# The low parts of the query, key and value weight splits: from GpSimd to VectorE

## The chip, the cores and the metric

The kernel runs on one core of one Trainium2 chip. The metric is the device time of one execution in microseconds, from runs on the chip; one further execution was taken with the hardware profiler, and every row below is from it. Engines are named as in the profile: PE is TensorE, PEld its weight loads, DVE is VectorE, ACT is ScalarE, POOL is GpSimd, SP is SyncE.

## The reference, cut to what matters

A decoder trunk of two layers on 512 tokens of width 1024, all in float32. Each layer is a mixer (three kinds of attention on 16 heads of 64) and a mixture of experts (32 experts, top 2 in one group of 8).

```python
for l in range(DEPTH):
    mod = cond @ ada_w[l] + ada_b[l]                      # six vectors of 1024
    h = rmsnorm(x, norm1_g[l]) * (1.0 + sc1) + sh1
    u = h @ w_in[l]                                       # queries, keys, values, gates
    o_a, o_b, o_c = nsa(...), fox(...), stick_breaking(...)
    x = x + g1 * (rmsnorm_per_head(concat(o_a, o_b, o_c)) @ w_out[l])
    h = rmsnorm(x, norm2_g[l]) * (1.0 + sc2) + sh2
    x = x + g2 * hier_moe(h, ...)
```

The change touches only `h @ w_in`. The kernel makes that product in split form: each float32 matrix is written as a high part (rounded to the `fp32r` type) and a low part (the difference), and three matmuls (high by high, high by low, low by high) replace one.

## The kernel before, in words

**Stages of a layer.** First `ln1` (line 530) normalizes x, transposes it on PE and splits it into `h` (high and low). Then the mixer runs a list of steps written out by hand, `ORDER` (one string for each layer, lines 102 to 105). A step is half a query/key projection (`q0` to `q7`, `proj_qk`, line 597), half a value projection (`v0` to `v2`, `proj_v`, line 675), one unit of an attention (`sb`, `fox`, `nsa`), a piece of the modulation (`ada`), or a piece of the output projection (`p..`, `w..`, `t.`). Projections and attention units are interleaved, so that PE has matmuls while ACT and DVE work on an attention unit. After the mixer comes the mixture of experts (`experts`, line 1315), which streams 1 MB weight tiles.

**How an engine's order comes about.** The framework orders the instructions of each engine when the program is built, from the order in which the code emits them and from what they depend on. Each engine then runs its own list strictly in that order: an instruction that waits for a semaphore holds all that stand behind it on its engine.

**The split of a weight.** `split` (line 282) makes the high part with a cast, on ACT by default (line 283), and the low part with a subtraction, on DVE by default (line 284; `le` names another engine). Line 284 is therefore the line of every low part in the profile, and the tile names tell them apart: `wl` are the low parts of the query/key weights (`split_qk`, line 583), `vl` those of the value weights (`split_v`, line 637), `wol` those of the output weights (`wo_parts`, line 1090), `h` those of the normalized input, `q`, `k`, `hilo` and `oh` others. A projection step of `qk` needs two pairs (`wh`, `wl`) of 128x512; a value projection needs four pairs (`vh`, `vl`) of 128x512. All of them take turns in 8 buffers of the tag `W`, so a cast into a buffer waits until PE has read what lay there. The split for the second half of a projection is emitted right behind the first half's matmuls (line 611), one step ahead of its use.

In the kernel before, `wl` is made on DVE only for `q7` and `q6` of the first layer and `vl` on DVE only for `v2` of the first layer; all the others are made on POOL. POOL also makes the low parts `wol` (always) and half of the `h` (line 564), one multiplication of the rotary embedding (line 626), and some additions of the modulation (line 382).

**An attention unit.** `scores` (line 790, matmuls on line 797) writes S in PSUM, in one of two double banks. For `sb` (line 1008) follow three ACT passes (lines 1018 to 1020), a DVE operation that reads S (line 1021), two DVE scans (line 1023), a DVE subtraction that reads S again (line 1025) and an ACT pass (line 1026). For `fox` and `nsa`, `softmax` (line 816) is a DVE maximum, ACT exponentials and DVE scalings. Then PE transposes the result (line 864) and ACT or DVE copies it out of PSUM (lines 278, 280).

Of the kernel before, what the change touches and what calls it, by code (L numbers as in the profile page):

```python
# [113 lines left out]
class K:  # L114
# [468 lines left out]
    def split_qk(self, l, c, s, he=None, le=None):  # L583
        w = self.get("wqk", l, c)[:, s]
        parts = []
        for h in range(2):
            wh = self.t4("W", [128, 4, 128], F32R, "wh")
            wl = self.t4("W", [128, 4, 128], F32R, "wl")
            self.split(wh, wl, w[:, 4 * h:4 * h + 4, :], he=he, le=le or (self.nc.vector if l == self.layers[0] and c > 5 else self.nc.gpsimd))
            parts.append((wh, wl))  # L590
        if s:
            self.done("wqk", l, c)
        return parts
# [43 lines left out]
    def split_v(self, l, g):  # L637
        parts = []
        for j in range(0, NK, 2):
            w = self.get("wv", l, g)  # L640
            if l != self.layer:
                x = self.t4("L", [128, 2, 2, 256], F32R, "vhl")
                wh, wl = x[:, 0], x[:, 1]
            else:
                wh = self.t4("W", [128, 2, 256], F32R, "vh")
                wl = self.t4("W", [128, 2, 256], F32R, "vl")
            he = None
            le = self.nc.vector if g == 2 and l == self.layers[0] else self.nc.gpsimd
            self.split(wh, wl, w[:, j:j + 2, :], he=he, le=le)
            parts.append((wh, wl))  # L650
        self.done("wv", l, g)
        return parts
# [999 lines left out]
```

## Time and profile before

| What | us |
|---|---|
| device time, median of 3 runs | 1844.76 |
| the three runs | 1836.57, 1845.58, 1844.76 |
| the profiled execution, device time | 1839.93 |
| its span, first to last instruction | 1838.0 |
| mean granted TensorE clock, of full speed | 0.965 |

How to read what follows: a busy time is the sum of an engine's own instructions; a wait is idle time of an engine just before an instruction, put down to the instruction whose semaphore came last. The granted clock is a share of full speed; this chip grants two levels, 1.2 and 2.4 GHz, which the table of stages shows as 0.5 and 1.0 where a stretch has one of them alone.

### The profile page before, as it was taken

The page shows a single profiled execution, that of the slowest core. Times are in us where ns is not written, and L with a number is a line of the kernel's source. Part 1 is how long each engine was busy: PE and PEld are TensorE (multiplying, and loading weights), DVE is VectorE, ACT ScalarE, POOL GpSimd, SP SyncE. Part 2 cuts the span into 40 slices and gives each one's busy share as a digit, 9 for nine tenths or more (in the row PEclk, how much of TensorE's full clock was granted, in tenths as well). Part 3 has the DMA queues.
Part 4 walks back from the last instruction along what each step waited for, and adds up shares of the span by engine and source line. Part 5 has one row for each costly group of instructions (what it writes and reads, how often), then busy time and mean ns, then how long its engine had stood idle before and what let it go on. Part 6 is the DMA issues. An engine that isn't in the chain of part 4 may idle for free. (4 is left out here: it accounts for less than half of the span.)

```text
span 1838.0 us, 24077 instructions
## 1 busy us (share of the span) xinstructions
PE 1742.5 (95%) x9126; PEld 917.2 (50%) x9126; DVE 970.0 (53%) x2022; ACT 663.1 (36%) x1526; POOL 235.3 (13%) x193
## 2 busy tenths in 40 slices
PE   6999999998999999999989999999979999999996
PEld 3766755655333433333356776566533343333333
DVE  2465367767344444333374975777634444344335
ACT  3565434345322222222245543445532222222222
POOL 1341412110000000000043332211000000000000
PEclk8998999999999999999999999899989999999998
DMA  7522374314999999999933244411399999999994
GB/s 293 208 92 90 113 292 153 123 46 176 384 420 420 419 420 420 420 421 420 419 144 138 91 141 151 157 62 53 149 354 411 419 420 421 420 420 420 420 421 196
DMA packets 78823, 512.64 MB, mean 279 GB/s; under 512 B 11000, under 2 KB 12280, under 8 KB 20080
## 3 DMA queue, kind: packets, MB, share of 16 engines
q1 hardware_dynamic: 72336, 496.77, 67.1%
q0 software_dynamic: 5216, 10.09, 1.5%
q10 hardware_dynamic: 1152, 4.19, 0.6%
q8 instruction: 75, 1.23, 0.3%
q14 instruction: 44, 0.36, 0.1%
HBM read 512.05 MB, written 6.29 MB: 282 GB/s over the span
## 5 line engine op out<-in xcount | busy, mean ns | idle before, releaser
L1387 PE MATMUL up<-ring_w,xeT 128*64 128x512 f32 x2048 | 461.7, 599 | 8.8 <-DMA ring_w<-in_expert_w 8.7
L1387 PEld LDWEIGHTS up<-ring_w,xeT 128*64 128x64 f32 x2048 | 139.2, 137 | 298.3 <-issue 250.7
L1417 PE MATMUL down<-ring_w,hT 128*64 128x512 f32 x1024 | 247.5, 605 | 0.8 <-DMA ring_w<-in_expert_w 0.8
L1395 ACT ACTIVATE F<-up,small 128x512 f32<-128x512 f32 x64 | 44.0, 687 | 461.1 <-PE up L1387 447.9
L609 PE MATMUL pj<-h,wh 128*128 128x512 f32 x512 | 167.1, 407 | 0.0
L466 DVE TENSOR_TENSOR x<-x,sc 128x512 f32<-128x512 f32 x256 | 159.3, 683 | 3.5 <-PE sc L1448 3.3
L1440 DVE TENSOR_SCALAR S<-sb,cf 128x512 fp32r<-128x512 f32 x64 | 47.9, 751 | 204.4 <-PE sb L1438 203.5
L283 ACT CAST Yh<-us 64x512 fp32r<-64x512 f32 x128 | 79.1, 618 | 197.4 <-DVE us L1428 189.7
L1362 POOL DMA_INDIRECT xr<-rows,index x32 | 31.9, 996 | 748.5 <-PE xg L1371 708.0
L1448 PE MATMUL sc<-Yh,S 128*128 128x512 f32 x256 | 110.2, 431 | 8.8 <-ACT z L1499 8.8
L797 PE MATMUL S<-k,q 64*128 64x512 f32 (+3 forms) x576 | 106.4, 399 | 8.5 <-DVE sbc L1025 5.2
L1417 PEld LDWEIGHTS down<-ring_w,hT 128*64 128x64 f32 x1024 | 62.2, 136 | 101.6 <-issue 87.6
L609 PEld LDWEIGHTS pj<-h,wh 128*128 128x128 f32 x512 | 96.1, 192 | 23.2 <-issue 1.2
L824 ACT ACTIVATE Pm<-S,sm_m 128x128 f32<-128x128 f32 (+3 forms) x160 | 83.0, 525 | 62.9 <-DVE sm_m L821 59.5
L1428 DVE TENSOR_TENSOR us<-down,gb 128x512 f32<-128x512 f32 x64 | 44.3, 692 | 116.3 <-PE down L1417 116.3
L1448 PE MATMUL sc<-Yl,S 128*128 128x512 f32 x256 | 103.7, 405 | 0.0
L609 PE MATMUL pj<-h,wl 128*128 128x512 f32 x256 | 102.5, 403 | 0.0
L1375 ACT ACTIVATE xeT<-xg,mods 128x128 f32<-128x128 f32 x256 | 95.5, 460 | 10.2 <-PE xg L1371 10.2
L284 POOL TENSOR_TENSOR wl<-ring_wqk,wh 128x512 fp32r<-128x512 f32 x56 | 74.8, 1349 | 167.1 <-ACT wh L283 161.3
L284 DVE TENSOR_TENSOR Yl<-us,Yh 64x512 fp32r<-64x512 f32 x128 | 87.3, 682 | 2.0
L821 DVE TENSOR_REDUCE sm_m<-S 128x2 f32<-128x256 f32 (+3 forms) x80 | 65.4, 820 | 36.7 <-PE S L797 35.8
L1448 PEld LDWEIGHTS sc<-Yh,S 128*128 128x128 f32 x256 | 49.6, 194 | 67.7 <-issue 58.3
(332 smaller groups left out, 2612.8 us busy)
## 6 DMA issues: line engine op xcount, KB each, us to landing
ring_w<-in_expert_w SPq DMA_DIRECT2D x384, 1024.0 KB, 19.8
ring_ada_sc<-in_ada_w SPq DMA_DIRECT2D x16, 1024.0 KB, 4.8
ring_ada_sh<-in_ada_w SPq DMA_DIRECT2D x16, 1024.0 KB, 5.3
ring_ada_g<-in_ada_w SPq DMA_DIRECT2D x16, 1024.0 KB, 4.8
ring_wqk<-in_wqk SPq DMA_DIRECT2D x16, 1024.0 KB, 6.7
ring_wv<-in_wv SPq DMA_DIRECT2D x6, 1024.0 KB, 4.8
rows<-nx ACTq DMA_DIRECT2D x8, 512.0 KB, 2.6
x<-in_x SPq DMA_DIRECT2D x4, 512.0 KB
```

Of the source, the lines that this page charges most:

```text
L283: (he or self.nc.scalar.copy)(hi, x)
L284: (le or self.nc.vector).tensor_sub(lo, x, hi)
L466: self.nc.vector.tensor_add(x, x, p)
L609: nc.tensor.matmul(p, x[:, k % 4, :], self.h[k][:, y, :], start=k == 0 and i == 0, stop=k == NK - 1 and i == 2)
L797: nc.tensor.matmul(s[:, b, :n], q[r, x, 128 * i:128 * i + 128], k[r, y, :n], start=j == 0, stop=j == 2)
L821: nc.vector.tensor_reduce(m[:, 0:2], s[:, :, :n], AX, OP.max, negate=True)
L824: nc.scalar.activation(p[:, j, :n], s[:, j, :n], AF.Exp, bias=m[:, j:j + 1], accum_out=m[:, 2 + j:3 + j])
L1375: nc.scalar.activation(XE[pr][:, k, :], p[:, 128 * i:128 * i + 128], AF.Identity, scale=mods[:, 8 + k:9 + k], bias=mods[:, k:k + 1])
L1387: pe(nc.tensor.matmul(p[64 * b:64 * b + 64, :], XE[pr][:, k, 64 * o:64 * o + 64], w[:, b if o else 1 - b, kk, :], start=k == 0, stop=k == ...
L1417: pe(nc.tensor.matmul(p[64 * b:64 * b + 64, :], H[e][:, f, :], w[:, f % 2, 512 * c:512 * c + 512], start=f == 0, stop=f == 3, skip_group_c ...
L1440: nc.vector.tensor_scalar(s, p, self.cf[:, C_PM:C_PM + 1], None, op0=OP.is_equal)
L1448: pe(nc.tensor.matmul(p, ST[pr, c][:, 128 * t:128 * t + 128], Y[pr][j][:, c, :], start=j == 0, stop=j == 1))
```

## The change

`split_qk` no longer names an engine for the low part unless its caller does, and `split_v` never does, so `split` falls back to its default, DVE. The casts on ACT stay. The low parts `wol` and `h` on POOL stay.

```diff
@@ -586,7 +586,7 @@
         for h in range(2):
             wh = self.t4("W", [128, 4, 128], F32R, "wh")
             wl = self.t4("W", [128, 4, 128], F32R, "wl")
-            self.split(wh, wl, w[:, 4 * h:4 * h + 4, :], he=he, le=le or (self.nc.vector if l == self.layers[0] and c > 5 else self.nc.gpsimd))
+            self.split(wh, wl, w[:, 4 * h:4 * h + 4, :], he=he, le=le)
             parts.append((wh, wl))
         if s:
             self.done("wqk", l, c)
@@ -645,8 +645,7 @@
                 wh = self.t4("W", [128, 2, 256], F32R, "vh")
                 wl = self.t4("W", [128, 2, 256], F32R, "vl")
             he = None
-            le = self.nc.vector if g == 2 and l == self.layers[0] else self.nc.gpsimd
-            self.split(wh, wl, w[:, j:j + 2, :], he=he, le=le)
+            self.split(wh, wl, w[:, j:j + 2, :], he=he)
             parts.append((wh, wl))
         self.done("wv", l, g)
         return parts
```

## Rows read from the trace of the kernel before

**Rows 1.** The page, part 1: engine, busy us, share, instructions.

```profile
PE 1742.5 (95%) x9126; PEld 917.2 (50%) x9126; DVE 970.0 (53%) x2022; ACT 663.1 (36%) x1526; POOL 235.3 (13%) x193
```

**Rows 2.** By stage: length, busy us of PE, PEld, DVE, ACT, POOL, clock, DMA.

```profile
40.00:275.00 235.00, 224.27 (x1346) 160.61 (x1346) 124.76 (x249) 114.74 (x241) 68.19 (x49) 0.95 0.43 159
...
950.00:1150.00 200.00, 195.87 (x1199) 147.89 (x1199) 135.65 (x232) 97.44 (x206) 73.59 (x55) 0.97 0.36 128
```

**Rows 3.** PE's waits, 40 to 275 us: total us, times, longest.

```profile
PE S L797 <- DVE sbc L1025: 3.4, 1, 3.4
...
PE cmp_p L749 <- DVE X L742: 1.9, 1, 1.9
PE T L976 <- DVE cp L972: 1.4, 1, 1.4
```

**Rows 4.** PE's waits, 936 to 1150 us.

```profile
PE S L797 <- DVE sbc L1025: 1.8, 3, 1.2
...
PE pv L687 <- POOL vl L284: 0.8, 1, 0.8
```

**Rows 5.** Groups of POOL's low parts: busy us, mean ns | idle before, releaser.

```profile
L284 POOL TENSOR_TENSOR wl<-ring_wqk,wh 128x512 fp32r<-128x512 f32 x56 | 74.8, 1349 | 167.1 <-ACT wh L283 161.3 <-PE pj L609 5.8
...
L284 POOL TENSOR_TENSOR vl<-ring_wv,vh 128x512 fp32r<-128x512 f32 x20 | 30.4, 1532 | 57.6 <-ACT vh L283 57.6
```

**Rows 6.** Tile `wl`, DVE: ns min/median/max, first and last start, form.

```profile
L284 DVE TENSOR_TENSOR wl<-ring_wqk,wh x8: 691/693/1226, 50.7 to 69.1; 128x512 fp32r<-128x512 f32 x8
```

**Rows 7.** POOL's `wl`, then `vl`, in the first stage: length, busy us (instructions), clock, DMA.

```profile
40.00:275.00 235.00, 31.96 (x24) 0.95 0.43 159
...
40.00:275.00 235.00, 11.37 (x8) 0.95 0.43 159
```

**Rows 8.** POOL in order of time, first layer: start, us, instruction.

```profile
103.95 6.36 POOL L284 TENSOR_TENSOR wl<-ring_wqk,wh 128x512 fp32r<-128x512 f32 x4
```

**Rows 9.** DVE in order of time, first layer.

```profile
104.50 3.46 DVE L1023 TENSOR_TENSOR_SCAN sbc<-cf,Pm 128x384 f32<-128x384 f32 x2
...
135.56 1.81 DVE L1023 TENSOR_TENSOR_SCAN sbc<-cf,Pm 128x384 f32<-128x384 f32 x2
```

**Rows 10.** POOL and DVE in order of time, second layer.

```profile
951.07 4.15 POOL L284 TENSOR_TENSOR vl<-ring_wv,vh 128x512 fp32r<-128x512 f32 x3
...
947.12 0.49 DVE L283 CAST h<-us 128x256 fp32r<-128x256 f32 x2
...
953.18 2.20 DVE L283 CAST h<-us 128x256 fp32r<-128x256 f32 x2
```

**Rows 11.** Who waited for PE's matmuls of line 609: us, times.

```profile
  ACT wh L283: 54.3, 27
```

**Rows 12.** DVE groups by form, whole trace: busy, mean ns | idle before, releaser.

```profile
L284 DVE TENSOR_TENSOR q<-us,q 128x512 fp32r<-128x512 f32 x16 | 12.5, 780 | 20.2 <-ACT q L283 20.0
...
L284 DVE TENSOR_TENSOR wl<-ring_wqk,wh 128x512 fp32r<-128x512 f32 x8 | 6.0, 759 | 11.8 <-ACT wh L283 11.8
```

**Rows 13.** PE in order of time, first layer: idle before and releaser in brackets.

```profile
118.49 0.58 PE L797 MATMUL S<-k,q 64*128 64x256 f32 x2 [3.40 <-DVE sbc L1025]
```

**Rows 14.** Second layer in slices of 25 us, columns as in Rows 2.

```profile
1025.00:1050.00 25.00, 25.00 (x138) 18.70 (x137) 22.53 (x32) 17.17 (x30) 9.85 (x7) 1.00 0.35 127
1050.00:1075.00 25.00, 24.10 (x186) 20.51 (x186) 22.01 (x32) 8.99 (x22) 10.48 (x7) 1.00 0.29 100
```

**Rows 15.** POOL's `wl`, then `vl`, by slice: busy us (instructions), clock, DMA.

```profile
1025.00:1050.00 25.00, 4.35 (x3) 1.00 0.35 127
...
1025.00:1050.00 25.00, 3.70 (x3) 1.00 0.35 127
1050.00:1075.00 25.00, 9.20 (x6) 1.00 0.29 100
```

**Rows 16.** Granted clock in stretches behind PE's waits: length, PE busy, clock.

```profile
117.10:124.00 6.90, 5.51 (x21) 0.51 0.01 2
...
1011.40:1018.20 6.80, 6.08 (x20) 0.50 0.00 0
```

## The prediction

> **What bounds the kernel now.** I read the page's busy shares first: PE is at work for 95% of the span, DVE 53%, POOL 13% [rows 1]. An average over a mixer and an expert stage says little of a mixer edit, so next the table of stages, cut so that the moved subtractions lie inside it [rows 2]. In 40 to 275 us (first layer) PE is busy for 224.3 of 235 us at 0.95 of full clock; in 950 to 1150 us (second layer) for 195.9 of 200 at 0.97. So PE sets the time there, and what DVE can win or lose is small: PE's idle time of 10.7 and 4.1 us, and the clock's loss of 0.05 x 235 = 11.8 and 0.03 x 200 = 6.0 us, 32.6 us in all. Then PE's waits: the largest that DVE ends are for the stick-breaking unit (3.4 us), the compression (1.9 and 1.4) [rows 3] and 1.8 us in the second layer; a low part made by POOL is waited for once, 0.8 us [rows 4].
>
> **What goes from POOL.** 56 `wl` and 20 `vl`, 74.8 and 30.4 us busy [rows 5]. POOL is idle for long times before them, waiting for ACT's cast, so its own time was free; only the 0.8 us wait ends. I take -0.8 us. What else stands in POOL's queue (the rotary multiplication, the `h` and `wol` subtractions) starts earlier or at the same time; no DMA is moved.
>
> **What comes to DVE.** The same subtraction on DVE has a median of 0.693 us [rows 6]. 76 x 0.693 = 52.7 us, of which 24 `wl` and 8 `vl` lie in the first stage [rows 7] and the other 44 in the second, one of them just before 950 us: 22.2 and, with 43, 29.8 us. DVE has 110 us idle in the first and 64 in the second, so nothing need be added to the sum from busy time alone.
>
> **What DVE gets back.** While POOL runs these subtractions, DVE's own operations take longer. Two scans of 384 took 3.46 us beside four POOL subtractions and 1.81 us elsewhere [rows 8, 9], 0.41 us lost for each; two casts took 2.20 us beside three of them and 0.49 us at another place [rows 10], 0.57 us for each. These are places that I picked as stretched, so 0.57 x 76 = 43 us is one end and 0 the other; I take half of the milder pair, 0.21 us for each, 16 us, because most subtractions run where DVE is idle. The net load is +37 us.
>
> The Trainium skill, SBUF — State Buffer, section on the two separate sides, says that a VectorE instruction with two SBUF inputs and a GpSimd one that reads SBUF exclude each other for a whole instruction. The stretched scans agree. If each of the 76 met one such instruction half-way, an estimate by that rule would be 0.5 x 1.35 x 76 = 51 us back, and DVE's net load about nothing. The sum goes by the rows.
>
> **What of it reaches PE.** The moved instruction waits for ACT's cast, and the cast for PE to leave a buffer: ACT's casts waited for PE's projection matmuls 27 times, 54.3 us [rows 11]. On POOL nobody stood behind that wait. On DVE the attention unit's scans and copies do. The low parts already on DVE show the size: 11.8 us idle before 8 `wl`, 20.0 before 16 `q` [rows 12], so 31.8 / 24 = 1.3 us each, mostly where DVE had nothing else to do. The price of one is between 0 (it falls into idle time) and 1.3 + 0.69 us (all in front of the unit that PE waits for).
>
> I cost it by how full DVE gets. Net load by stage: 22.2 - 32 x 0.21 = 15.5 and 29.8 - 43 x 0.21 = 20.8 us. The ratio of DVE's busy to its idle time goes from 124.8 / 110.2 = 1.13 to 140.3 / 94.7 = 1.48, +31%; in the second stage from 135.7 / 64.3 = 2.11 to 156.5 / 43.5 = 3.60, +71%. I let the waits that DVE ends grow by as much: 6.7 x 0.31 = 2.1 and 1.8 x 0.71 = 1.3 us; and the share of the clock's loss that goes with them, 11.8 x 6.7 / 10.7 x 0.31 = 2.3 and 6.0 x 1.8 / 4.1 x 0.71 = 1.9 us. Together +7.6 us. This scaling is a choice, not a row; its ends are 0 and the rival below.
>
> Against it stands one chain that POOL does hold up. The scans at 104.5 us end 1.65 us late; the exponential of that unit waits for what DVE does next [rows 9], and PE's wait of 3.4 us, which ends at 118.49, is for a later unit of the same chain [rows 13]. I give back the 1.65 us and half of it for the clock, -2.5 us in all, though the four subtractions may land in the same place on DVE and keep it.
>
> **The sum.** -0.8 + 7.6 - 2.5 = +4.3 us. The profiled execution took 1839.93 us, 4.8 below the median; the four executions shown average 1841.7, and I start from that: 1841.7 + 4.3 = 1846.0 us. A change within 0.5% (9.2 us) counts as none, which is about what a measurement of this kernel can tell: 1835.5 to 1854.0. The forecast is no change, with a lean to slower.
>
> **Rival, slower: DVE fills up in the second layer.** In 1025 to 1075 us DVE is busy for 22.53 and 22.01 of 25 us [rows 14], 5.5 us idle in all, and 12 of the moved subtractions lie there [rows 15]: 8.3 us, less 12 x 0.21 = 2.5 given back, 5.8 us. That alone fills it. Each wait for a cast (1.3 us) is then time that the attention units lose: 12 x 1.3 = 15.6 us, and PE falls dry behind them, with one stretch at half clock such as the 6.8 us at 0.50 from 1011 us on [rows 16], 3.4 us. Together +19 us, 1861. It decides as soon as a subtraction stands at the head of DVE's queue before its cast is done, since nothing is left to absorb it. Against it: PE is busy for 49.1 of these 50 us [rows 14], so it has projection matmuls to run while the units are late. Chance 0.31.
>
> The Trainium skill, Perfetto Trace Analysis, Optimizing Scalar/DVE Operations, says that with a saturated VectorE it may make sense to give work to GpSimd, and this edit does the reverse. These two slices are where the rule could apply; over the whole stage DVE is at 68%, and it would not.
>
> **Rival, faster: the units get their DVE back.** If the subtractions fall into idle time and POOL's hold was the main cost, the waits at 118 us (3.4), for `vl` (0.8) and the longest for DVE's subtraction in the second layer (1.2) go [rows 4, 13], and with them the stretches at half clock behind them, 6.9 and 6.8 us [rows 16], 6.8 us gained. -12 us, 1830. For it: the stretched scans. Against it: only 1.65 us of the chain before 118 us is POOL's, and the four POOL subtractions there end at 110.3 us, 8 us before the wait does [rows 8]. Chance 0.14.
>
> That the change does not do what it says I leave out: both call sites pass no engine, and the default is DVE.
>
> **How the numbers follow.** No change 0.55, slower 0.31, faster 0.14. The range reaches most of the way to both rivals: 1833 leaves out the full gain, 1866 takes in the slower case and 5 us on it for the bound of the casts' waits. Outside it I leave about 0.08 below and 0.10 above.
>
> **What would show it.** Right: POOL's groups `wl` and `vl` gone; 76 more DVE instructions at 0.69 to 0.8 us; the 384 scans of the first layer near 1.8 us for two; DVE's idle time before `wl` and `vl` large, ended by ACT's casts; PE busy in the two stages within 5 us of before; the expert stages of the same length. Wrong, slower: PE's waits for the stick-breaking subtraction, for exponentials or for copies out of PSUM grow to over 10 us in 975 to 1150 us, with more half-clock stretches. Wrong, faster: the wait at 118 us is gone and the stretch behind it is at full clock. Were a time outside the range to come with equal mixers, the experts' weight stream would be the place to look.

## The result, and the profile after

| | before | after |
|---|---|---|
| median, us | 1845.17 (4 runs, 1836.57 to 1846.95) | 1833.47 (4 runs, 1832.07 to 1837.26) |
| ratio | 1 | 0.9948, interval 0.9926 to 0.9971 |
| span of the profiled execution, us | 1838.0 | 1830.2 |
| its mean granted clock | 0.965 | 0.970 |

The change made the kernel faster by 0.5% (11.7 us between the medians). 1846 had been forecast as no change with a lean to slower. 1833.5 lies outside the band that was to count as no change (1835.5 to 1854.0) and just inside the stated range (1833 to 1866), at its lower end, near the rival "the units get their DVE back" (1830).

The page, part 1, and the two stages (columns as in [rows 1] and [rows 2]), the changed kernel:

```profile
PE 1732.1 (95%) x9126; PEld 909.5 (50%) x9126; DVE 993.8 (54%) x2098; ACT 664.1 (36%) x1526; POOL 131.5 (7%) x117
...
40.00:275.00 235.00, 224.29 (x1375) 157.28 (x1371) 145.76 (x294) 118.16 (x252) 26.23 (x20) 0.97 0.43 161
950.00:1150.00 200.00, 194.84 (x1192) 143.74 (x1190) 142.88 (x279) 97.94 (x205) 11.15 (x8) 0.98 0.39 139
```

POOL lost 76 instructions, DVE gained 76. But DVE is busy for only 23.8 us more, 993.8 against 970.0 [rows 1]. In the same 235 us of the first layer PE finished 29 more matmuls (1375 against 1346 [rows 2]) with no more busy time; the clock is higher there (0.97 against 0.95). In the second layer there is no such gain.

DVE's groups by form in the changed kernel (busy us, mean ns | idle before). The change takes one line out of the code, so line numbers behind it are one lower than before:

```profile
L284 DVE TENSOR_TENSOR wl<-ring_wqk,wh 128x512 fp32r<-128x512 f32 x64 | 44.7, 706 | 52.1 <-ACT wh L283 49.8 <-PE T L863 2.1
L284 DVE TENSOR_TENSOR vl<-ring_wv,vh 128x512 fp32r<-128x512 f32 x24 | 16.2, 684 | 6.9 <-ACT vh L283 5.6 <-PE hn L1043 1.3
L284 DVE TENSOR_TENSOR q<-us,q 128x512 fp32r<-128x512 f32 x16 | 10.9, 684 | 3.6 <-ACT q L283 3.5
...
L1022 DVE TENSOR_TENSOR_SCAN sbc<-cf,Pm 128x384 f32<-128x384 f32 x8 | 7.2, 940 | 0.0
L1022 DVE TENSOR_TENSOR_SCAN sbc<-cf,Pm 128x256 f32<-128x256 f32 x8 | 6.4, 837 | 0.0
```

The same view of the kernel before:

```profile
L284 DVE TENSOR_TENSOR vl<-ring_wv,vh 128x512 fp32r<-128x512 f32 x4 | 2.5, 687 | 0.0
...
L1023 DVE TENSOR_TENSOR_SCAN sbc<-cf,Pm 128x256 f32<-128x256 f32 x8 | 10.5, 1348 | 0.1
L1023 DVE TENSOR_TENSOR_SCAN sbc<-cf,Pm 128x384 f32<-128x384 f32 x8 | 8.9, 1151 | 0.1
```

`wl` and `vl` on DVE grew from 6.0 [rows 12] and 2.5 to 44.7 and 16.2 us, so 52.4 us came. With 23.8 us more in all, 28.6 us went: DVE's other operations became shorter, the scans of 256 from 1348 to 837 ns, those of 384 from 1151 to 940, the `q` subtractions from 780 [rows 12] to 684. Put down to POOL's 76 subtractions, that is 28.6 / 76 = 0.38 us of DVE's time for each.

PE's waits, 40 to 275 us and then 936 to 1150 us, in the changed kernel:

```profile
PE S L796 <- DVE sbc L1024: 3.1, 1, 3.1
...
PE S L796 <- ACT Pm L823: 0.6, 1, 0.6
PE T L863 <- ACT Pm L1025: 0.6, 1, 0.6
...
PE px L704 <- ACT us L283: 2.5, 1, 2.5
PE pv L686 <- DVE vl L284: 2.5, 1, 2.5
PE pv L686 <- POOL h L284: 1.3, 1, 1.3
```

And one wait of before, 40 to 275 us, that the prediction passed over because DVE does not end it:

```profile
PE S L797 <- ACT Pm L824: 2.4, 1, 2.4
```

**Where the time went.** I took the same matmul in both timelines and subtracted its start before from its start after. At 52 us the difference is -2.8 us, at 113 us -2.7, at 133 us -3.8, at 155 us -10.3, at 160 us -9.5, at the first expert matmul of the first layer -8.8 (463.84 to 455.00), at the last one -8.7, at the first of the second layer -6.3 (1349.18 to 1342.84), at the end -7.8. So the first layer's gain comes in one place, between 133 and 160 us, and is 5.7 us there. The second layer gives back 2.4 us. The first 2.8 us are gone before the change has moved anything: the windows of the two executions show the granted clock there (before, then after):

```profile
24.90:31.70 6.80, 6.06 (x24) 1.81 (x24) 4.71 (x12) 2.92 (x9) 3.67 (x4) 0.50 0.90 341
```

```profile
24.90:31.70 6.80, 4.43 (x33) 2.16 (x33) 4.43 (x11) 4.25 (x11) 3.66 (x4) 1.00 1.03 395
```

The one runs this stretch at 1.2 GHz, the other at 2.4, with the same instructions in the same order on PE. The experiments below show this to be a matter of the execution, not of the kernel.

**The place.** The timeline of before, 127 to 145 us (start, us, engine, line; in brackets the idle time before and its releaser; the first line is for a later point):

```profile
108.00 0.96 DVE L1025 TENSOR_TENSOR sbc<-S,sbc 128x768 f32<-128x768 f32 x1
...
127.40 1.30 POOL L284 TENSOR_TENSOR vl<-ring_wv,vh 128x512 fp32r<-128x512 f32 x1 [17.10 <-ACT vh L283]
127.57 2.26 DVE L1023 TENSOR_TENSOR_SCAN sbc<-cf,Pm 128x256 f32<-128x256 f32 x2
...
136.43 2.01 POOL L284 TENSOR_TENSOR vl<-ring_wv,vh 128x512 fp32r<-128x512 f32 x1 [5.52 <-ACT vh L283]
137.28 1.70 DVE L284 TENSOR_TENSOR hilo<-sq,hilo 128x512 fp32r<-128x512 f32 x1
138.91 0.94 DVE L1025 TENSOR_TENSOR sbc<-S,sbc 128x768 f32<-128x768 f32 x1
139.89 0.84 ACT L1026 ACTIVATE Pm<-sbc 128x768 f32<-128x768 f32 x1 [3.54 <-DVE sbc L1025]
...
141.77 0.62 ACT L283 CAST k<-us 128x512 fp32r<-128x512 f32 x1
...
142.42 0.72 DVE L284 TENSOR_TENSOR k<-us,k 128x512 fp32r<-128x512 f32 x1 [2.56 <-ACT k L283]
143.06 0.41 DVE L821 TENSOR_REDUCE sm_m<-S 128x2 f32<-128x256 f32 x1
...
143.51 0.37 ACT L824 ACTIVATE Pm<-S,sm_m 128x128 f32<-128x128 f32 x1 [0.53 <-DVE sm_m L821]
144.37 0.58 PE L797 MATMUL S<-k,q 64*128 64x256 f32 x2 [2.39 <-ACT Pm L824]
```

The same instructions in the changed kernel:

```profile
123.73 1.27 DVE L1022 TENSOR_TENSOR_SCAN sbc<-cf,Pm 128x256 f32<-128x256 f32 x2
...
132.62 0.67 DVE L284 TENSOR_TENSOR hilo<-sq,hilo 128x512 fp32r<-128x512 f32 x1
133.20 0.95 DVE L1024 TENSOR_TENSOR sbc<-S,sbc 128x768 f32<-128x768 f32 x1
134.19 0.85 ACT L1025 ACTIVATE Pm<-sbc 128x768 f32<-128x768 f32 x1 [2.27 <-DVE sbc L1024]
...
137.72 0.37 ACT L823 ACTIVATE Pm<-S,sm_m 128x128 f32<-128x128 f32 x1 [0.59 <-DVE sm_m L820]
138.58 0.38 PE L796 MATMUL S<-k,q 64*128 64x256 f32 x2 [0.64 <-ACT Pm L823]
```

Read backwards from PE. Its wait of 2.39 us is for the exponential of a softmax unit (143.51). The exponential waits for DVE's maximum (143.06), which stands in DVE's queue behind a `k` subtraction (142.42); that one waits for ACT's cast of `k` (141.77), and the cast stands in ACT's queue behind the last pass of a stick-breaking unit (139.89). For that pass ACT sits idle for 3.54 us, until DVE's subtraction of line 1025 is done. DVE makes that one behind `hilo`, and `hilo` takes 1.70 us in place of 0.67 because POOL is at work on a `vl`. The pair of scans at 127.57 takes 2.26 in place of 1.27 for the same reason. Two holds of 1.0 us each, and the name that PE's wait carries is ACT's.

The durations show how the two engines keep each other out. POOL's subtraction at 136.43 takes 2.01 us, 0.7 us longer than the 1.30 of the one at 127.40: it starts while the second scan of [rows 9] (135.56, 1.81 us for two) is still running. `hilo` then takes until 138.98, 0.54 us beyond POOL's end at 138.44; unheld it takes 0.67 us. The Trainium skill, SBUF — State Buffer, section on the two separate sides, says that whichever starts first holds the shared ports for its whole instruction; this row agrees.

What stands behind the wait is worth more than the wait. The clock in the 10.2 us that follow, before and then after:

```profile
144.40:154.60 10.20, 10.20 (x48) 9.43 (x49) 6.27 (x12) 5.01 (x10) 0.00 (x0) 0.50 0.23 96
```

```profile
138.50:148.70 10.20, 9.56 (x76) 8.55 (x76) 8.41 (x16) 5.97 (x13) 0.00 (x0) 1.00 0.23 92
```

After the wait of 2.39 us PE runs at 1.2 GHz and makes 48 matmuls; after 0.64 us it stays at 2.4 GHz and makes 76 in the same time. The starts of the same matmuls show what each part is worth: between 141 and 144.4 us the difference grows by the 1.75 us of the shorter wait, from there to 154.7 us by another 4.6, while before runs at half clock. Then the changed kernel gives back 0.85 us, most of it in a wait of 0.6 us for ACT that before does not have (the line of `T` and `Pm` in the waits above). Net of that, and from 133 us on, it is 5.7 us.

### The profile page after: what moved, and what is told of

Its sections match the earlier page's. It is cut to its first block, busy times and chain, and to the rows that moved or that the text cites. A ratio compares the mean times of both kernels' runs of the same rounds, so it can differ in the third digit from the quotient of the medians.

```text
span 1830.2 us, 24036 instructions
## 1 busy us (share of the span) xinstructions
PE 1732.1 (95%) x9126; PEld 909.5 (50%) x9126; DVE 993.8 (54%) x2098; ACT 664.1 (36%) x1526; POOL 131.5 (7%) x117
## 5 line engine op out<-in xcount | busy, mean ns | idle before, releaser
L1374 ACT ACTIVATE xeT<-xg,mods 128x128 f32<-128x128 f32 x256 | 95.5, 461 | 10.1 <-PE xg L1370 10.1
L1354 DVE TENSOR_SCALAR index<-wc 128x1 int32<-128x1 f32 x32 | 7.1, 222 | 130.3 <-PE wc L1351 130.2
```

The source lines that it names most:

```text
L1374: nc.scalar.activation(XE[pr][:, k, :], p[:, 128 * i:128 * i + 128], AF.Identity, scale=mods[:, 8 + k:9 + k], bias=mods[:, k:k + 1])
```

## Experiments

Timed runs alternate with runs of the kernel before on the same chip, and each ratio is against these.

**Both kernels again.** No edit, so that the spread of each is known.

> The kernel before, unchanged, beside itself. It measures two things: what the comparison says of no change, and whether the stretches at half clock in the first 40 us (24.9 to 31.7 and 35.2 to 38.6 us in the trace of before, none in the trace of after, with the same order of instructions on PE there) come and go by themselves. Theory 'the clock of the first 40 us is a matter of the execution': ratio 1.000 within 0.003, and a trace whose start can look like either of the two; the runs spread over some 10 us. Rival 'the change brought the start its clock': the start shows the same half-clock stretches again, 10 us of them.

> The changed kernel, unchanged, once more. Theory: ratio 0.994 to 0.996 against before; in the trace the stretch from 110 to 155 us has one wait of about 3 us and at most 4 us at half clock, where before had 17 us at half clock. If the gain were only the first 40 us, a trace with half clock there would take about 1837 us and the ratio would be near 0.998.

Before against itself: 1.0001 (0.998 to 1.0022); its runs reach from 1832.6 to 1847.9 us, some 15 us, while those of the changed kernel stay between 1831.9 and 1838.0. The changed kernel again: 0.9970 (0.9954 to 0.9986). The gain is real, 0.3 and 0.5% by the two measurements; the second gain is smaller than the ratio of 0.994 to 0.996 that was expected for it. In the profile of before's second execution the wait at 145 us is 2.40 us and the 10.2 us at half clock are there; in the changed kernel's second one 0.66 us and none. The start went as the rival of the first expectation had it: 13.7 us at half clock in before's second profile, none in the changed kernel's. These two runs leave open whether the change touches the start; the table further down settles it.

**POOL makes the subtractions as well.** The changed kernel, with each of the 76 differences made once more on POOL, into a tile that nobody reads. DVE, PE and ACT have the instructions of the changed kernel in its order.

```diff
+    def held(self, x, hi):
+        t = self.M.tile(list(x.shape), BF, name="junk", tag="junk", bufs=1)
+        self.nc.gpsimd.tensor_sub(t, x, hi)
...
+            if not (l == self.layers[0] and c > 5):
+                self.held(w[:, 4 * h:4 * h + 4, :], wh)
...
+            if not (g == 2 and l == self.layers[0]):
+                self.held(w[:, j:j + 2, :], wh)
```

> The changed kernel, and beside each of the 76 moved subtractions POOL makes the same difference once more into a tile of bf16 that nobody reads. The orders of PE, DVE and ACT are those of the changed kernel, so only POOL's hold on DVE comes back. Theory 'the gain is DVE freed from POOL's hold': DVE's scans beside POOL's subtractions are stretched again (two of 384 at 2.5 us or more in place of 1.8), the waits of the units around 115 and 140 us return, and most of the 10 us goes: ratio 0.998 to 1.004. Rival 'the gain is the other order of the engines' instructions, or low parts that are ready 0.6 us sooner': ratio stays at 0.993 to 0.996, though DVE's operations are stretched.

1867.85 us, ratio 1.0146 (1.0118 to 1.0175). The page, and PE's waits in the second layer:

```profile
PE 1743.8 (93%) x9126; PEld 918.8 (49%) x9126; DVE 1046.2 (56%) x2098; ACT 663.9 (36%) x1526; POOL 252.4 (14%) x193
...
PE pv L694 <- DVE vl L284: 6.2, 1, 6.2
PE pv L694 <- POOL h L284: 5.3, 2, 2.7
```

The time went beyond the expected ratio of 0.998 to 1.004, so this run costs more than the holds that were to come back. No instruction reads what POOL makes here (a cast into one of the `W` buffers and a weight transfer now wait for POOL's reading too); still DVE's 2098 instructions take 1046.2 us in place of 993.8, 0.69 us for each of the 76, and the time rises by 32 us over the changed kernel (1867.85 against 1836.26 in its second measurement, on the same chip). So POOL's subtractions by themselves, read by nobody, lengthen DVE's work. `hilo` is back at 1.71 us, PE's wait for the exponential at 149.9 us is 3.38 us, and the 10.2 us at half clock are behind it again. (The wait is 1.0 us longer than before's because POOL here also holds the `k` subtraction of that chain, 1.75 us at 146.89 in place of 0.72.) How much of the 32 us is the hold, how much those waits, and how much the `h` subtractions that now stand behind the added ones in POOL's queue (the last line), this run does not separate.

**One layer at a time.** The default engine in the first layer only (first diff, against the changed kernel), then in the second only.

```diff
-            self.split(wh, wl, w[:, 4 * h:4 * h + 4, :], he=he, le=le)
+            self.split(wh, wl, w[:, 4 * h:4 * h + 4, :], he=he, le=le or (self.nc.vector if l == self.layers[0] else self.nc.gpsimd))
-            self.split(wh, wl, w[:, j:j + 2, :], he=he)
+            self.split(wh, wl, w[:, j:j + 2, :], he=he, le=self.nc.vector if l == self.layers[0] else self.nc.gpsimd)
```

```diff
-            self.split(wh, wl, w[:, 4 * h:4 * h + 4, :], he=he, le=le)
+            self.split(wh, wl, w[:, 4 * h:4 * h + 4, :], he=he, le=le or (self.nc.vector if l != self.layers[0] or c > 5 else self.nc.gpsimd))
-            self.split(wh, wl, w[:, j:j + 2, :], he=he)
+            le = self.nc.vector if g == 2 or l != self.layers[0] else self.nc.gpsimd
+            self.split(wh, wl, w[:, j:j + 2, :], he=he, le=le)
```

> Low parts on DVE in the first layer only, the second layer as before. From the two traces, the first layer's mixer became shorter by some 10 us (2.8 of them before 40 us) and the second layer's longer by 2. Theory 'the gain is that of the first layer': ratio 0.992 to 0.995, the same as the change or a little better. Rival 'both layers gain, the traces differ by chance': ratio 0.997, half of the gain.

> Low parts on DVE in the second layer only, the first as before. Theory 'in the second layer DVE fills up, as the slower rival of the prediction had it, but for a few us': PE waits 2.5 to 3.5 us for a vl of DVE near 1045 us, the second layer's mixer is 3 to 5 us longer than that of before, ratio 1.001 to 1.003. Rival 'the second layer is neutral': ratio within 0.001 of 1, no wait for vl.

First layer only: 0.9954 (0.9936 to 0.9972), about -8.5 us. Second layer only: 1.0015 (0.9995 to 1.0035), about +2.8 us and not told apart from nothing. The sum, -5.7 us, fits the changed kernel's two measurements (-9.6 and -5.5 by their ratios). So the first layer holds the gain, and the second at best nothing. The wait for a `vl` that the second expectation named is there, 2.46 us at 1047.99.

**Which four.** Four `vl` of the first layer: moved alone in the kernel before (first diff), or left alone on POOL in the changed one (second).

```diff
-            le = self.nc.vector if g == 2 and l == self.layers[0] else self.nc.gpsimd
+            le = self.nc.vector if g > 0 and l == self.layers[0] else self.nc.gpsimd
```

```diff
-            self.split(wh, wl, w[:, j:j + 2, :], he=he)
+            self.split(wh, wl, w[:, j:j + 2, :], he=he, le=self.nc.gpsimd if g == 1 and l == self.layers[0] else None)
```

> The kernel before with only four of the 76 subtractions moved: the vl of v1 in the first layer, which POOL made at 127 to 142 us. The orders of PE and ACT are those of before, and DVE's has four more entries. Theory 'these four hold the chain whose end PE waits for at 144 us': the wait there falls from 2.4 us to about 0.6, the 10 us at half clock behind it go, 2 + 5 = 7 us, ratio 0.996 to 0.997. Rival 'the gain needs the whole change (order of the engines, other holds)': the wait stays over 2 us and the ratio is 0.999 to 1.001.

> The changed kernel with those four subtractions left on POOL. The orders of PE and ACT are those of the changed kernel. Theory of the four: the wait of over 2 us and some 10 us at half clock come back behind it, and the ratio to before is 1.000 to 1.003, since the second layer's loss of 3 to 4 us stays. Rival 'the gain is spread over all': ratio 0.996 to 0.998.

These two moved the wrong four, by my error: the expectation puts `v1`'s at the place at 128 to 142 us, but the program makes `v1` first, at 82 to 92 us, and the four at the place are `v0`'s. With `v1`'s alone on DVE: 1.0002 (0.9983 to 1.0021), the wait 2.40 us. With all but `v1`'s on DVE: 0.9975 (0.9961 to 0.9988), the wait 0.65 us. They say nothing on the place, but they serve as a control: these four, elsewhere in the same layer, are worth nothing that can be measured. The next two take the right four in the same two ways.

```diff
-            le = self.nc.vector if g == 2 and l == self.layers[0] else self.nc.gpsimd
+            le = self.nc.vector if g != 1 and l == self.layers[0] else self.nc.gpsimd
```

```diff
-            self.split(wh, wl, w[:, j:j + 2, :], he=he)
+            self.split(wh, wl, w[:, j:j + 2, :], he=he, le=self.nc.gpsimd if g == 0 and l == self.layers[0] else None)
```

> The kernel before with four low parts on VectorE in place of GpSimd: the vl of v0 in the first layer, which lie at 128 to 142 us in the profile of before (the eight vl that the earlier expectation called v1's are v1's at 82 to 92 us and v0's here). TensorE's order is that of before. Theory A (GpSimd holds the unit whose exponential TensorE waits for at about 144 us, and the half-clock stretch of 10.24 us stands behind that wait): the wait falls from 2.4 to 0.6 to 1.0 us, the stretch of 10.24 us that begins at 144.4 is gone, the first stage (start to first expert matmul) 4 to 8 us shorter than in a run of before with the same start-up stretches, ratio 0.996 to 0.998. Theory B (the gain of the first layer is spread over all 32 subtractions, and the wait at 144 us is set by all that comes before it): wait 2.0 us or more, the stretch stays, ratio 0.999 to 1.001. Theory C (four subtractions on VectorE in front of that unit cost as much as the hold): wait of 3 us or more, ratio above 1.001.

> The changed kernel with only the four vl of v0 in the first layer left on GpSimd. TensorE's order is that of the changed kernel. Theory A (that one place carries the first layer's larger part): the wait at about 144 us is back at 2 us or more with the 10.24 us at half clock behind it; the first stage 4 to 8 us longer than in the changed kernel; ratio 0.998 to 1.001. Theory B (the gain is spread): wait 0.6 to 1.0 us, no stretch, ratio 0.995 to 0.997 as the changed kernel itself.

Four of the 76, moved alone: 0.9952 (0.9931 to 0.9972). The other 72, moved without them: 0.9999 (0.998 to 1.0018). The timeline and the window behind the wait, first of the four alone, then of the 72:

```profile
132.71 0.67 DVE L284 TENSOR_TENSOR hilo<-sq,hilo 128x512 fp32r<-128x512 f32 x1
...
138.73 0.38 PE L797 MATMUL S<-k,q 64*128 64x256 f32 x2 [0.55 <-ACT Pm L824]
...
138.60:148.80 10.20, 9.56 (x76) 8.56 (x76) 8.42 (x16) 5.97 (x13) 0.00 (x0) 1.00 0.20 81
```

```profile
106.16 1.79 DVE L1022 TENSOR_TENSOR_SCAN sbc<-cf,Pm 128x384 f32<-128x384 f32 x2
...
108.45 0.94 DVE L1024 TENSOR_TENSOR sbc<-S,sbc 128x768 f32<-128x768 f32 x1
...
137.45 1.72 DVE L284 TENSOR_TENSOR hilo<-sq,hilo 128x512 fp32r<-128x512 f32 x1
...
144.55 0.39 PE L796 MATMUL S<-k,q 64*128 64x256 f32 x2 [2.40 <-ACT Pm L823]
...
144.80:155.00 10.20, 10.20 (x50) 9.60 (x49) 6.50 (x12) 4.76 (x10) 0.00 (x0) 0.50 0.21 86
```

This settles where the gain is: as far as intervals of some 0.2% to either side can tell, it comes with these four and goes with them. (Two more of its lines, from 106 us on, are read further down.)

**Which of the four.** The third (beside `hilo`) alone, then the first two (beside the scans of 256) alone.

```diff
-            le = self.nc.vector if g == 2 and l == self.layers[0] else self.nc.gpsimd
+            le = self.nc.vector if l == self.layers[0] and (g == 2 or g == 0 and j == 4) else self.nc.gpsimd
```

> The kernel before with one low part moved: the third of v0's four in the first layer, which GpSimd makes at 136.43 us for 2.01 us while VectorE's subtraction hilo takes 1.70 us in place of 0.67. Orders of TensorE and ScalarE are those of before. Theory A (the held hilo delays the stick-breaking subtraction behind it, the ScalarE exponential that waits for that, and all that ScalarE does for the next unit): hilo 0.67 us, TensorE's wait at about 144 us falls by 1.0 us from 2.39 to about 1.4; if the 10.24 us at half clock behind it shrink with the wait, ratio 0.997 to 0.999, and if they stay, 0.999 to 1.000. Theory B (the first two, beside the scans, carry it): the wait stays above 2.0 us, ratio 0.999 to 1.001.

> The kernel before with the first two of v0's four low parts of the first layer moved (at 127.40 and 129.27 us in before; the pair of scans of 256 beside the first takes 2.26 us in place of 1.27). The third and fourth stay on GpSimd, and hilo stays held. ScalarE makes one exponential of the stick-breaking unit later in its order. Theory A (both holds lie on the chain to the wait at about 144 us, 1.0 us each): the wait falls by up to 1.0 us, to about 1.4; ratio 0.997 to 0.999 if the half-clock stretch shrinks with it. Theory B (only the hold of hilo counts, as the scans' delay is absorbed at ScalarE's wait behind them): the wait stays above 2.0 us, ratio 0.999 to 1.001. Theory C (the first two alone carry the whole gain): wait below 1.0 us, no stretch, ratio 0.995 to 0.997.

In the edit of the second run the last condition is `j < 4`. The third alone: 0.9979 (0.9962 to 0.9996). The first two alone: 0.9963 (0.9945 to 0.9981). The timelines, in this order:

```profile
124.25 2.06 DVE L1023 TENSOR_TENSOR_SCAN sbc<-cf,Pm 128x256 f32<-128x256 f32 x2
...
133.76 0.67 DVE L284 TENSOR_TENSOR hilo<-sq,hilo 128x512 fp32r<-128x512 f32 x1
...
139.81 0.53 PE L797 MATMUL S<-k,q 64*128 64x256 f32 x2 [1.57 <-ACT Pm L824]
```

```profile
129.22 1.27 DVE L1023 TENSOR_TENSOR_SCAN sbc<-cf,Pm 128x256 f32<-128x256 f32 x2
...
137.47 1.73 DVE L284 TENSOR_TENSOR hilo<-sq,hilo 128x512 fp32r<-128x512 f32 x1
...
144.59 0.38 PE L797 MATMUL S<-k,q 64*128 64x256 f32 x2 [1.65 <-ACT Pm L824]
```

Each hold, taken away alone, shortens the wait by 0.7 to 0.8 us, and both together by 1.84. The clock does not follow in proportion. Behind 1.57 us the stretch at half clock is still 10.2 us long, behind 1.65 it is 6.8, behind 0.55 there is none. With the third alone, the wait accounts for only 0.8 us of a measured 3.9 (0.7 to 7.0 by the interval); with the first two, 0.7 us of wait and 1.7 of clock for a measured 6.8 (3.5 to 10.1). By the starts of the same matmuls, from 133 to 160 us, the two are worth 1.0 and 2.4 us, and the four together 5.8. What the rest of the two gains is stays open; for the four together the 5.8 us lie inside the interval (5.2 to 12.7).

All fourteen profiled executions in one table, read from their timelines and clock records (us; "start" is time at half clock in the first 60 us, "at 118" that in 110 to 130 us, "behind" that in the 11 us behind the wait; the last column, mixer 2, runs from the end of the first layer's last matmul of line 1387 to the start of the second layer's first one):

| kernel | `hilo` | wait | behind | start | at 118 | first expert matmul | mixer 2 |
|---|---|---|---|---|---|---|---|
| before | 1.70 | 2.39 | 10.2 | 10.2 | 6.8 | 463.8 | 430.4 |
| before again | 1.71 | 2.40 | 10.2 | 13.7 | 6.8 | 468.7 | 428.3 |
| second layer only | 1.71 | 2.40 | 10.2 | 0 | 3.4 | 459.8 | 433.5 |
| `v1` alone | 1.71 | 2.40 | 10.2 | 13.7 | 6.8 | 468.9 | 427.7 |
| all but `v0` | 1.72 | 2.40 | 10.2 | 10.2 | 6.8 | 468.9 | 431.9 |
| POOL as well | 1.71 | 3.38 | 10.2 | 10.2 | 10.2 | 475.0 | 451.4 |
| `v0`, third | 0.67 | 1.57 | 10.2 | 0 | 3.4 | 463.6 | 433.2 |
| `v0`, first two | 1.73 | 1.65 | 6.8 | 13.7 | 6.8 | 462.6 | 432.4 |
| `v0` alone | 0.67 | 0.55 | 0 | 0 | 3.4 | 458.5 | 427.3 |
| after | 0.67 | 0.64 | 0 | 0 | 3.4 | 455.0 | 432.8 |
| after again | 0.67 | 0.66 | 0 | 0 | 3.4 | 453.4 | 432.4 |
| first layer only | 0.67 | 0.65 | 0 | 10.2 | 6.8 | 457.5 | 427.4 |
| all but `v1` | 0.67 | 0.65 | 3.4 | 13.7 | 6.8 | 459.4 | 432.7 |
| `v` on POOL in layer 2 | 0.67 | 0.67 | 0 | 13.7 | 6.8 | 458.4 | 426.0 |

The wait follows the holds in every row. The stretches at half clock in the first 60 us, and the one at 118 us, do not follow the edits: "first layer only" and "`v` on POOL in layer 2" have the changed kernel's first layer and 10.2 and 13.7 us at the start, "second layer only" has that of before and none. A look at one pair of profiles would have put 2.8 us of them down to the change.

The last two columns carry such differences too. The two profiles of before, the same program, are 0.6 us apart at 282 us and 4.8 us apart at the first expert matmul, with 13.7 and 27.3 us at half clock between 425 and 480 us. And mixer 2 follows its own time at half clock: 34 to 41 us where it is 426.0 to 428.3 us long, 44 to 49 us where it is 430.4 to 433.5 (without the run with POOL's extra work). So differences of 4 us in these columns are not an effect of an edit by themselves.

**The second layer.** The changed kernel, with eight `vl` of the second layer (`v0`, `v1`) left on POOL.

```diff
-            self.split(wh, wl, w[:, j:j + 2, :], he=he)
+            self.split(wh, wl, w[:, j:j + 2, :], he=he, le=self.nc.gpsimd if g < 2 and l != self.layers[0] else None)
```

> The changed kernel with the vl of v0 and v1 of the second layer left on POOL (8 of the 76). Theory 'the second layer loses at the vl that stand at the end of a full DVE queue': the wait of 2.5 to 3.5 us near 1043 us goes, the second layer's mixer is about 3 us shorter than with the change, ratio to before 0.994 to 0.996. Rival 'POOL's hold on DVE there costs as much as the wait': ratio 0.997 as with the change.

0.9970 (0.9955 to 0.9986), as the changed kernel run again, and the number of the expectation's rival. The window and the timeline of the changed kernel show what the eight do there:

```profile
1015.00:1045.00 30.00, 27.54 (x157) 21.12 (x156) 28.78 (x48) 18.71 (x34) 2.87 (x2) 0.99 0.28 107
...
1042.94 0.68 DVE L284 TENSOR_TENSOR vl<-ring_wv,vh 128x512 fp32r<-128x512 f32 x1
...
1043.68 0.38 PE L686 MATMUL pv<-vl,h 128*128 128x256 f32 x1 [2.46 <-DVE vl L284]
```

DVE is busy for 28.8 of 30 us, and PE waits 2.46 us for a `vl` that stands in DVE's queue behind the work of two attention units and of the rotary embedding. With the eight on POOL waits of 0.23 and 0.47 us for `vl` are left of it, and mixer 2 is 426.0 us long, against 431.9 to 433.5 in the five executions with all of the second layer on DVE. But the same program of the second layer as before also took 427.3 to 433.2 us in seven executions, so the 3 us between the means (432.7 and 429.5) are a size, not a proof. Whether the eight gain anything is open. No version tried beats the changed kernel clearly: "first layer only" (0.9954) and "`v0` alone" (0.9952) are as good.

## Why the prediction was wrong, point by point

- **What bounds the kernel**: right. PE sets the time, and what could be won lay in waits and clock. The gain stayed below the ceiling of 32.6 us.
- **The list of waits**: this is the step that failed. I listed the waits that DVE ends by name and left out the 2.4 us that ACT ends, as if a hold on DVE could not reach it. ACT's exponential was late because DVE's subtraction ahead of it was late, and that because of POOL. The runs showed that wait at 2.39 us before and 0.64 after, with 10.2 us at half clock behind it that went too: 5.7 us by the starts of the same matmuls, where the sum had nothing. [rows 9] itself shows the scans (135.56) that stand directly in front of the held `hilo`; I used that row as the unstretched example, which it is, and did not read the instruction behind it.
- **What DVE gets back**: 16 us taken, 28.6 us measured (0.38 for each against 0.21; the milder pair of rows gave 0.41). Halving the pair was the mis-sized step. By the rule that the prediction took from the Trainium skill (SBUF — State Buffer, the two separate sides) the estimate was 51 us; the measurement lies between.
- **The cost of net load, +7.6 us**: the scaling of DVE's waits with its ratio of busy to idle was the failed term. By layer it was 2.1 + 2.3 = +4.4 and 1.3 + 1.9 = +3.2 us. The first layer gave about -8.5 us: not more waiting in proportion to load, but one held chain set free. The second came out near its number, +2.4 by the aligned starts and +2.8 (-0.9 to +6.4) with that layer alone; that is luck as far as the runs show, since the same program's mixer 2 varies by 6 us with its clock, and the largest new waits there are 2.5 us for a `vl` and 2.5 us for ACT, not those that the term scaled. A mean load does not tell which operation is late.
- **The one held chain, -2.5 us**: the mechanism, but in the wrong place. The scans at 104.5 us did fall to 1.79 us. But two of the four moved subtractions landed in front of them and one behind them, and the first of these (at 103.01 us with 72 moved) took 1.76 us in place of 0.68 beside POOL's additions to `ada_s`. So with 72 subtractions moved the unit's subtraction starts at 108.45 us, where it had started at 108.00 before (timelines of "all but `v0`" and of before, above); 0.36 of the 0.45 us is the start of that execution, and nothing is gained. The wait at 118 us, 3.40 us in [rows 13] and 3.3 to 3.4 in the other executions with POOL at work there, went to 3.0 or 3.1, and the clock behind it was at half for 6.8 or 3.4 us with kernels of either kind (table). The caveat given with the term, that DVE may keep what POOL gives up, is what happened.
- **POOL's wait of 0.8 us**: gone by name, but PE waits 1.3 us for POOL's `h` in the changed kernel, so nothing was won.
- **The slower rival** named the place and the mechanism rightly (DVE full in the second layer, PE waiting for a `vl` behind the units) but priced each of twelve subtractions at 1.3 us, 15.6 us. One wait of 2.46 us came; the two waits of 1.2 and 1.3 us at 1010 us are gone, and one of 2.5 for ACT at 996 us is new. For the rest of the twelve no wait shows, as the counterargument had it: PE had other matmuls meanwhile.
- **The faster rival** was the right kind, priced at -12 and given 0.14. Its named places (118 us, the two in the second layer) were not the ones, so that 1833.5 comes near its 1830 is luck.
- **The band of no change**: 1835.5 to 1854.0 stands around the median 1844.76, while the sum starts from 1841.7; around that start it would be 1832.5 to 1850.9. The measured ratio decides: its interval (0.9926 to 0.9971) leaves out no change.
- **Signs to look for**: the groups on POOL, the 76 instructions at 0.68 to 0.71 us, PE's busy time within 1.1 us in both stages and the idle time before `wl` (52.1 us) ended by ACT's casts came as written; before `vl` it is only 6.9 us. "The wait at 118 us is gone" was given as the sign of faster, and faster came without it.

## What to carry to other kernels

A wait's releaser is the last link, not the cause: before leaving a wait out of an account, follow the releasing engine's queue back until an instruction is found that takes longer than its like elsewhere. Where POOL and DVE both read two tensors from SBUF, compare each group's shortest and mean durations, and look at what stands behind a stretched one. Here two holds of 1.0 us in front of a unit that PE waited for, with a stretch at half clock behind the wait, were worth the whole gain, while moving the other 72 subtractions was worth nothing that could be measured. An edit of 76 instructions can stand on four of them, so move those four alone first.

## What was not expected

- The start of the program runs at 1.2 GHz for 10 to 14 us in nine of fourteen profiled executions and not at all in five, with kernels of each kind in both sets; the stretch at 118 us was 3.4 us long in those five and 6.8 in eight of the nine (10.2 in the run with POOL's extra work). Timed runs of before spread over some 15 us and those of the changed kernel over some 6. The spread goes with the clock: of before's 12 repeated runs the longest, 1847.4 us, had a mean granted clock of 0.960 and the shortest, 1832.6 us, 0.970. Whether it is the start that makes the difference is not shown, since only profiled executions record where the clock fell.
- Behind waits of 1.57 and 1.65 us PE spent 10.2 and 6.8 us at half clock, behind 0.55 to 0.67 us none in five of six executions (3.4 in one). So in the profiles the last microsecond of the wait frees far more of the clock than the first one; the timed ratios of the two half edits (0.9979 and 0.9963) do not show such a difference.
- POOL's extra subtractions, read by nobody, cost DVE 0.69 us each, nearly twice the 0.38 us that the same subtractions cost in the kernel before.
